# One operand of 512 columns for the high and low input parts in every second feed-forward group, and PSUM banks handed out in pairs

## The chip, the cores and the metric

The kernel runs on one core of a Trainium2 chip. The metric is the device time of one execution in microseconds (us), the median of several runs.

## The reference

Two layers of a decoder trunk with a residual h of 256 positions and 1024 channels. Each layer mixes positions in four branches, gates them and adds them to h, then runs a gated feed-forward part of 2816 channels with a causal convolution of three taps, and then adds a gated projection of a second input. Cut to what matters here:

```python
for i in range(DEPTH):                              # DEPTH = 2
    xn = rms_norm(h, norm_mix[i])
    u = xn @ w_in[i]                                # split into the inputs of four branches
    ...
    h = h + mixed @ w_out[i]
    f = causal_dwconv(rms_norm(h, norm_ffn[i]) @ w_up[i], conv_f_w[i], conv_f_b[i])   # 3 taps
    f_gate, f_val = jnp.split(f, 2, axis=-1)        # 2816 channels each
    h = h + (jax.nn.silu(f_gate) * f_val) @ w_down[i]
    e = rms_norm(p[i] @ w_ple_in[i], ple_norm[i])
    g = jax.nn.sigmoid(rms_norm(h, ple_gate_norm[i]) @ w_ple_gate[i])
    h = h + g * e
```

## The kernel before, in words

All products are matmuls in a 32-bit format with fewer bits than float32. To come near float32 each operand is split in two parts, high and low, and each product is three matmuls: high weight by high input, high weight by low input, low weight by high input. The function `mm3` (L298) issues them on L305, L306 and L307, 256 columns each where the positions are the moving columns, and `tok_unit` (L345) on L348 to L350, 512 columns each where the weights move.

The weights come from memory in pieces of 128 x 1024. `take` hands them out in the order in which they are used, three pieces ahead. ScalarE makes the high part of a piece (L232) and VectorE the low part (L233); six buffers hold split pieces, so that the high part of a new piece waits until TensorE has done with the piece six before it.

The feed-forward part has 22 groups of 128 channels for the gate and as many for the value. The loop over `g2` (L1148 on) takes two groups at a time, `q` is the group in it and `s_` chooses gate or value. `chan_unit` computes one 128x256 output with 8 x 3 = 24 matmuls, and the two outputs of a group share one PSUM bank of 512 float32 columns, a tile of `mmbank` named mm. Four such banks go round. A group's bank is evacuated by two ScalarE copies with scale and bias (L1158, the last tap of the convolution) and four VectorE products that add the other two taps (L1164). Then come a Silu (L1167) and a product (L1168), and the result is split into high and low parts (L291, L292) for the next matrix product.

The first four groups of a layer, the early ones (EARLY = 4), are computed before the scale of the norm is known; `nrm.scaled` (L479) multiplies their banks by it afterwards into SBUF, and the evacuation reads from there.

Nobody writes the order of the instructions out. The program is traced in the order of the Python code, a scheduler then orders the instructions on each engine, and semaphores are placed for each dependence. A tile is the unit of such a dependence on a buffer that is used again: whoever takes the buffer next waits until everything that reads the old tile is done.

Other places that the change touches: `evac_a` (the first branch's convolution, which is also scaled by L479), the key of the sparse branch's indexer (a unit of 40 channels, copied on L1051 and transposed on L1055), and `tok_parts` (the last product of the kernel, in three parts, each followed by a tanh on L1203).

Of the kernel before, what the change touches and what calls it, by code (L numbers as in the profile page):

```python
# [129 lines left out]
def decoder_kernel(ctx: ExitStack, tc: tile.TileContext, w_dram, x_dram, xt_dram, p_dram, vec_dram, row_dram,  # L130
# [10 lines left out]
    RAW_BUFS, SPLIT_BUFS, LEAD, NBIG = 5, 6, 3, 43  # L141
# [12 lines left out]

    def st(shape, tag, bufs=1, dtype=F32):
        return sm.tile(shape, dtype, name=nm("s"), tag=tag, bufs=bufs)

    def mmbank():
        return ps.tile([P, 2, S], F32, name=nm("mm"), tag="mm", bufs=4)
# [127 lines left out]
    def split(dst, src, scale=1.0):  # L287

        hi, lo = dst
        if scale == 1.0:  # L290
            A.activation(hi, src, AF.Copy)  # L291
            V.tensor_tensor(lo, src, hi.bitcast(F32), op=ALU.subtract)  # L292
        else:
            A.activation(hi, src, AF.Copy, scale=scale)
            V.scalar_tensor_tensor(lo, src, scale, hi.bitcast(F32), op0=ALU.mult, op1=ALU.subtract)

    def mm3(out, wl, xs, c0, first, last):
# [3 lines left out]
        for k in range(nk):  # L301
            xh, xl = xs[k]
# [5 lines left out]

    def ktiles(pairs):
        return [(pairs[k // 2][0][:, k % 2, :], pairs[k // 2][1][:, k % 2, :]) for k in range(2 * len(pairs))]  # L310
# [9 lines left out]
    def chan_banks(nb, nrm):  # L320


        banks = [mmbank() for _ in range(nb)]
        ws = take(2 * nb)
        for k0 in (0, KD // 2):
# [3 lines left out]
            for i, bank in enumerate(banks):  # L329
# [6 lines left out]
    def tok_unit(xk, npieces, after={}):  # L336


        outs = [mmbank().rearrange("p a b -> p (a b)") for _ in range(2)]
# [61 lines left out]
    class Norm:  # L401
# [11 lines left out]
        def split(self, i, src, js=(0, 1)):  # L413

            if 0 in js:
                self.xs.append((bt(dtype=F32R), bt(dtype=F32R)))
            hi, lo = self.xs[i]
# [143 lines left out]
    for l in range(L):  # L561
# [45 lines left out]
        else:  # L607
            bbanks = [mmbank() for _ in range(2)]
# [9 lines left out]
        xsk = ktiles(nrm.xs)  # L618
        for c in range(len(bbanks), 4):
            bank = mmbank()  # L620
# [44 lines left out]
        def side_d():  # L665
# [111 lines left out]
            od = [(bt(dtype=F32R), bt(dtype=F32R)) for _ in range(2)]  # L777
# [43 lines left out]
        def side_c():  # L821
# [94 lines left out]
            oc = [(bt(dtype=F32R), bt(dtype=F32R)) for _ in range(2)]  # L916
# [40 lines left out]
        def side_a():  # L957
            oa = []
            o_pairs[0] = oa
            for i in range(2):  # L960
# [24 lines left out]
                hl = (bt(dtype=F32R), bt(dtype=F32R))  # L985
# [20 lines left out]
        def side_b():  # L1006
# [13 lines left out]
            for i in range(2):  # L1020
# [5 lines left out]
                hl = (bt(dtype=F32R), bt(dtype=F32R))  # L1026
# [11 lines left out]
        for fn in (evac_a, evac_ga):  # L1038
            for i in range(2):
                bank = mmbank()  # L1040
# [7 lines left out]
        bank = mmbank()  # L1048
# [33 lines left out]
        def turn_mixed(n):  # L1082
            for i in range(2):
# [5 lines left out]
                hl = (bt(dtype=F32R), bt(dtype=F32R))  # L1089
# [54 lines left out]
        fk = ktiles(nrm.xn())  # L1144
        for g2 in range(NG // 2):
            cf = st([P, 4, S], "e4", 2)
            pair = bt()
            for q in range(2):  # L1148
                g = 2 * g2 + q
                if g < EARLY:  # L1150
                    bank = nrm.scaled(early[g])
                else:
                    bank = mmbank()
# [15 lines left out]
            hl = (bt(dtype=F32R), bt(dtype=F32R))  # L1169
            split(hl, pair)  # L1170
            hid.append(hl)
# [137 lines left out]
```

## Time and profile before

| | before |
|---|---|
| median of 3 runs | 1031.39 us (1031.32 to 1031.87) |
| the profiled execution's own time | 1031.66 us |
| its span | 1029.9 us |
| TensorE busy | 1023.2 us, 99% |
| VectorE busy | 832.9 us, 81% |
| ScalarE busy | 691.0 us, 67% |
| granted TensorE clock | 1.000 |

The span is the time from the first to the last instruction of the profiled execution; its own time is a little longer than that. Busy times are sums of the durations of instructions. The matmuls of TensorE overlap, so its busy share says that it always had work, not how fast the work went. In the profile PE is TensorE, DVE VectorE, ACT ScalarE, POOL GpSimd and SP the engine that issues the transfers.

### The profile page before, as it was taken

Reading aid. Unit: us, or ns where it says so; the run is one execution under the profiler, and the core shown is the slowest. Engines: PE = TensorE matmul, PEld = TensorE weight load, DVE = VectorE, ACT = ScalarE, POOL = GpSimd, SP = SyncE. Lnnn points to the kernel's source line nnn. Section 1 sums busy time; section 2 is a strip of 40 time slices with the busy share of each in tenths; the row PEclk is TensorE's granted clock in tenths of the full one; section 3 lists DMA queues with packets and bytes.
Section 4 is the critical chain, followed back from the end, with each engine's and each line's share of the span. In section 5 each row is a group of like instructions: output and inputs, shape, how many; then the busy total and the mean of one; then the engine's idle time right before and its main releaser. Section 6 shows DMA issues by size and latency. Waiting matters only on the chain.

```text
span 1029.9 us, 16561 instructions
## 1 busy us (share of the span) xinstructions
PE 1023.2 (99%) x6124; PEld 901.0 (87%) x6124; DVE 832.9 (81%) x1526; ACT 691.0 (67%) x1190; POOL 0.2 (0%) x4
## 2 busy tenths in 40 slices
PE   9999999999999999999999999999999999999998
PEld 9988878887889999988899887888888899999887
DVE  7898999977869988765676989999688899877454
ACT  8688685977467766554766886868774676665443
POOL 0000000000000000000000000000000000000000
PEclk9999999999999999999999999999999999999999
DMA  8665844553538566476553656445446465665551
GB/s 290 231 207 167 269 142 144 184 164 107 211 101 308 159 204 192 144 259 188 186 176 124 213 172 216 141 148 179 147 137 210 144 205 178 188 186 183 191 160 41
DMA packets 53936, 185.30 MB, mean 180 GB/s; under 512 B 6112, under 2 KB 7904, under 8 KB 53856
## 3 DMA queue, kind: packets, MB, share of 16 engines
q1 hardware_dynamic: 53712, 184.25, 55.7%
q8 instruction: 48, 0.79, 0.3%
q14 instruction: 32, 0.26, 0.1%
q10 hardware_dynamic: 144, 0.00, 0.0%
HBM read 183.18 MB, written 1.05 MB: 179 GB/s over the span
## 4 chain that ended last, share of the span: by engine, by line
PE 96%; ACT 2%; DVE 1%; DMA 1%; SPq 0%; issue 0%; ACTq 0%
PE mm L348 18%; PE mm L349 18%; PE mm L350 18%; PE mm L307 11%; PE mm L305 11%; PE mm L306 11%; PE mm L371 1%; PE sp L439 1%; PE sp L873 1%; PE sp L729 1%; PE sp L789 1%; PE sp L903 1%; DMA raw<-in_w_dram 1%; ACT b L921 0%; ACT hi L232 0%; PE sp L847 0%
## 5 line engine op out<-in xcount | busy, mean ns | idle before, releaser
L232 ACT ACTIVATE hi<-raw 128x1024 fp32r<-128x1024 f32 (+1 forms) x342 | 354.9, 1048 | 210.8 <-PE mm L350 126.6
L233 DVE TENSOR_TENSOR lo<-raw,hi 128x1024 fp32r<-128x1024 f32 (+1 forms) x342 | 410.0, 1207 | 102.1 <-ACT hi L232 99.7
L348 PE MATMUL mm<-hi,b 128*128 128x512 f32 x848 | 337.5, 399 | 0.1
L349 PE MATMUL mm<-lo,b 128*128 128x512 f32 x848 | 331.1, 391 | 0.0
L350 PE MATMUL mm<-hi,b 128*128 128x512 f32 x848 | 330.2, 390 | 0.0
L305 PE MATMUL mm<-b,hi 128*128 128x256 f32 x976 | 276.5, 285 | 0.5 <-ACT hi L232 0.3
L307 PE MATMUL mm<-b,lo 128*128 128x256 f32 x976 | 275.7, 283 | 0.2 <-DVE lo L233 0.2
L306 PE MATMUL mm<-b,hi 128*128 128x256 f32 x976 | 275.7, 283 | 0.0
L348 PEld LDWEIGHTS mm<-hi,b 128*128 128x128 f32 x848 | 159.2, 188 | 35.8 <-issue 1.8
L350 PEld LDWEIGHTS mm<-hi,b 128*128 128x128 f32 x848 | 159.2, 188 | 33.7
L305 PEld LDWEIGHTS mm<-b,hi 128*128 128x128 f32 x976 | 186.8, 192 | 1.4 <-DVE b L428 0.6
L307 PEld LDWEIGHTS mm<-b,lo 128*128 128x128 f32 x976 | 186.9, 192 | 0.6 <-DVE lo L233 0.6
L306 PEld LDWEIGHTS mm<-b,hi 128*128 128x128 f32 x976 | 187.0, 192 | 0.3 <-DVE b L429 0.2
L349 PEld LDWEIGHTS mm<-lo,b 128*128 128x128 f32 x848 | 159.5, 188 | 31.5 <-issue 0.5
L1002 DVE SCALAR_TENSOR_TENSOR b<-s,vec,b 128x256 f32<-128x256 f32 x240 | 105.4, 477 | 0.0
L1164 DVE SCALAR_TENSOR_TENSOR s<-mm,vec,s 128x255 f32<-128x255 f32 (+1 forms) x144 | 59.7, 473 | 6.0 <-ACT s L1158 6.0
L291 ACT ACTIVATE b<-b 128x512 fp32r<-128x512 f32 x40 | 25.0, 626 | 21.8 <-DVE b L1168 19.1
L1158 ACT ACTIVATE s<-mm,vec 128x256 f32<-128x256 f32 x72 | 36.2, 553 | 2.7 <-PE mm L307 2.7
L292 DVE TENSOR_TENSOR b<-b,b 128x512 fp32r<-128x512 f32 x40 | 27.4, 687 | 12.6 <-ACT b L291 12.6
L479 DVE TENSOR_TENSOR b<-mm,s 128x512 f32<-128x512 f32 x24 | 16.3, 684 | 11.1 <-PE mm L307 11.0
L1167 ACT ACTIVATE s<-s 128x256 f32<-128x256 f32 x44 | 17.8, 410 | 9.7 <-DVE s L1164 9.6
L882 ACT ACTIVATE s<-sp,s,s 128x128 f32<-128x128 f32 (+1 forms) x32 | 16.0, 513 | 12.5 <-DVE s L878 6.2
(224 smaller groups left out, 779.4 us busy)
## 6 DMA issues: line engine op xcount, KB each, us to landing
raw<-in_w_dram SPq DMA_DIRECT2D x334, 512.0 KB, 4.2
raw<-in_w_dram SPq DMA_DIRECT2D x8, 256.0 KB, 4.6
b<-in_x_dram SPq DMA_DIRECT2D x8, 128.0 KB, 4.5
b<-in_lru_dram SPq DMA_DIRECT2D x4, 256.0 KB, 4.8
h<-in_xt_dram SPq DMA_DIRECT2D x4, 256.0 KB, 6.6
gain<-in_gain_dram SPq DMA_DIRECT2D x2, 512.0 KB, 6.1
out_dram<-h SPq DMA_DIRECT2D x3, 256.0 KB, 2.3
row<-in_row_dram SPq DMA_DIRECT2D x2, 272.0 KB, 5.4
```

Source lines behind the costliest of these rows:

```text
L232: A.activation(hi[:, cs], raw[:, cs], AF.Copy)
L233: last_lo[0] = V.tensor_tensor(lo[:, cs], raw[:, cs], hi[:, cs].bitcast(F32), op=ALU.subtract).ins
L292: V.tensor_tensor(lo, src, hi.bitcast(F32), op=ALU.subtract)
L305: T.matmul(out, a, xh, start=first and k == 0, stop=False)
L306: T.matmul(out, a, xl, start=False, stop=False)
L307: T.matmul(out, b, xh, start=False, stop=last and k == nk - 1)
L348: T.matmul(outs[b], xk[k][0][:, bs], wh[:, kk, :], start=k == 0, stop=False)
L349: T.matmul(outs[b], xk[k][0][:, bs], wl[:, kk, :], start=False, stop=False)
L350: T.matmul(outs[b], xk[k][1][:, bs], wh[:, kk, :], start=False, stop=last)
L1002: V.scalar_tensor_tensor(t, ypad[:, c, d:d + S], w[:, 31 * c + d:31 * c + d + 1], t, op0=ALU.mult, op1=ALU.add)
L1158: A.activation(cf[:, 2 * q + s_, :], bank[:, s_, :], AF.Identity, scale=w[:, 3 * c + 2:3 * c + 3], bias=bb[:, c:c + 1])
L1164: V.scalar_tensor_tensor(t, bank[:, s_, :S - d], w[:, 3 * c + 2 - d:3 * c + 3 - d], t, op0=ALU.mult, op1=ALU.add)
```

## The change

PSUM tiles for products are now pairs of banks: `mmbanks` returns the two halves of a tile of two banks and the tile itself, and two such tiles go round instead of four single banks. Every place that took banks now takes halves of pairs; two groups of the feed-forward part share a pair.

`two(True)` puts the high and low parts of an input side by side in one tile, so that they can move as one operand of 512 columns (128 x 2 x 256). From the third pass of the loop on, every second pass (g2 = 2, 4, 6, 8, 10) is `apart`: `mm3_apart` multiplies the high weight by the 512 columns into a whole bank (L322), the high input's product in its first half and the low input's in its second, and the low weight by the high input's 256 columns into the first half (L323). Two matmuls replace three. The two halves are added afterwards: ScalarE copies the second halves out of the pair (L1194), VectorE adds the first halves (L1195). In these passes ScalarE also makes the second tap's product (L1201), which one VectorE add per pass brings in (L1212); two VectorE products per group stay (L1206). `finish_group` runs Silu, product and split for both groups of a pass at once, and after the next pass's first group has been evacuated. Lines in the changed kernel: the weight pieces are split on L241 and L242, groups on L300 and L301, `mm3` is on L314 to L316, `tok_unit` on L364 to L366, `nrm.scaled` on L496, the copies with bias on L1198, the indexer's copy and transpose on L1070 and L1074.

```diff
-    RAW_BUFS, SPLIT_BUFS, LEAD, NBIG = 5, 6, 3, 43
+    RAW_BUFS, SPLIT_BUFS, LEAD, NBIG, NPAIR = 5, 6, 3, 36, 4
...
+    def two(paired=False):
+
+        if not paired:
+            return bt(dtype=F32R), bt(dtype=F32R)
+        t = big.tile([P, 2, 2, S], F32R, name=nm("b2"), tag="big2", bufs=NPAIR)
+        return t[:, 0], t[:, 1], t
...
-    def mmbank():
-        return ps.tile([P, 2, S], F32, name=nm("mm"), tag="mm", bufs=4)
+    def mmbanks():
+
+        t = ps.tile([P, 2, 2, S], F32, name=nm("mm"), tag="mm", bufs=2)
+        return t[:, 0], t[:, 1], t
...
+    def mm3_apart(out, wl, xs):
+
+        wh, wlo = wl
+        for k, (xh, _, xhl) in enumerate(xs):
+            T.matmul(out, wh[:, k, :], xhl, start=k == 0, stop=False)
+            T.matmul(out[:, 0, :], wlo[:, k, :], xh, start=False, stop=k == len(xs) - 1)
...
     def tok_unit(xk, npieces, after={}):
-        outs = [mmbank().rearrange("p a b -> p (a b)") for _ in range(2)]
+        outs = [flat(bank) for bank in mmbanks()[:2]]
...
         pcs = take(npieces)
+        halves = mmbanks()
         for b, c, n in ((0, 0, 512), (1, 0, 256), (1, 256, 256)):
-            bank = mmbank().rearrange("p a b -> p (a b)")[:, :n]
+            bank = flat(mmbanks()[0] if c == 0 and b == 0 else halves[c // 256])[:, :n]
...
                 V.tensor_tensor(xf, xf, self.rs2, op=ALU.mult)
-                hl = (bt(dtype=F32R), bt(dtype=F32R))
+                hl = two(True)
                 split(hl, xf)
...
         for fn in (evac_a, evac_ga):
+            both = mmbanks()
             for i in range(2):
-                bank = mmbank()
+                bank = both[i]
                 for j in range(2):
                     chan_unit(bank, j, xsk, 1)
                     pump()
...
-        bank = mmbank()
+        bank = mmbanks()[0]
         chan_unit(bank, 0, xsk, 1)
         t = st([40, S], "ikc", 1)
         A.activation(t, bank[0:40, 0, :], AF.Copy)
...
         for g in range(1, EARLY):
-            bank = mmbank()
+            if g % 2 == 0:
+                early += mmbanks()[:2]
             for s_ in range(2):
-                chan_unit(bank, s_, xsk, 1)
-            early.append(bank)
+                chan_unit(early[g], s_, xsk, 1)
         fk = ktiles(nrm.xn())
+
+        def finish_group(cf):
+            gv = cf.rearrange("p (q s) t -> p s q t", s=2)
+            sl, pair = bt(), bt()
+            A.activation(sl, gv[:, 0], AF.Silu)
+            V.tensor_tensor(pair, sl, gv[:, 1], op=ALU.mult)
+            hl = two()
+            split(hl, pair)
+            hid.append(hl)
+
+        waiting = None
         for g2 in range(NG // 2):
+            apart = 2 * g2 >= EARLY and g2 % 2 == 0
             cf = st([P, 4, S], "e4", 2)
-            pair = bt()
+            t1 = st([P, 4, S], "e4d", 2) if apart else None
             for q in range(2):
                 g = 2 * g2 + q
                 if g < EARLY:
-                    bank = nrm.scaled(early[g])
+                    u = nrm.scaled(early[g])
                 else:
-                    bank = mmbank()
+                    if apart or q == 0:
+                        banks = mmbanks()
                     for s_ in range(2):
-                        chan_unit(bank, s_, fk, 1)
+                        if apart:
+                            mm3_apart(banks[s_], take(1)[0], fk)
+                        else:
+                            chan_unit(banks[q], s_, fk, 1)
+                    u = banks[q]
+                if apart:
+                    u = bt()
+                    A.activation(u, banks[2][:, :, 1, :], AF.Copy)
+                    V.tensor_tensor(u, banks[2][:, :, 0, :], u, op=ALU.add)
                 for s_ in range(2):
                     c = g + s_ * NG
-                    A.activation(cf[:, 2 * q + s_, :], bank[:, s_, :], AF.Identity, scale=w[:, 3 * c + 2:3 * c + 3],
+                    A.activation(cf[:, 2 * q + s_, :], u[:, s_, :], AF.Identity, scale=w[:, 3 * c + 2:3 * c + 3],
                                  bias=bb[:, c:c + 1])
-                for d in (1, 2):
+                    if apart:
+                        A.activation(t1[:, 2 * q + s_, :], u[:, s_, :], AF.Copy, scale=w[:, 3 * c + 1:3 * c + 2])
+                for d in (2,) if apart else (1, 2):
                     for s_ in range(2):
                         c = g + s_ * NG
                         t = cf[:, 2 * q + s_, d:]
-                        V.scalar_tensor_tensor(t, bank[:, s_, :S - d], w[:, 3 * c + 2 - d:3 * c + 3 - d], t,
+                        V.scalar_tensor_tensor(t, u[:, s_, :S - d], w[:, 3 * c + 2 - d:3 * c + 3 - d], t,
                                                op0=ALU.mult, op1=ALU.add)
-                sl = st([P, S], "tb", 2)
-                A.activation(sl, cf[:, 2 * q, :], AF.Silu)
-                V.tensor_tensor(pair[:, q, :], sl, cf[:, 2 * q + 1, :], op=ALU.mult)
-            hl = (bt(dtype=F32R), bt(dtype=F32R))
-            split(hl, pair)
-            hid.append(hl)
+                if waiting is not None:
+                    finish_group(waiting)
+                    waiting = None
+            if apart:
+                V.tensor_tensor(cf[:, :, 1:], cf[:, :, 1:], t1[:, :, :S - 1], op=ALU.add)
+            waiting = cf
+        finish_group(waiting)
```

TensorE, before, at the border of two groups in the steady part of the first layer's feed-forward loop. mm_3764 is the bank of a group, mm_3834 that of the next one; hi and lo are the two parts of a weight piece.

```order
L306 MATMUL mm_3764<-b_3557,hi_3690 128x256
L307 MATMUL mm_3764<-b_3556,lo_3691 128x256
L305 MATMUL mm_3834<-b_3541,hi_3720 128x256 [waits DVE_49,Activation_49]
L306 MATMUL mm_3834<-b_3542,hi_3720 128x256
L307 MATMUL mm_3834<-b_3541,lo_3721 128x256
```

The next group begins in another of the four banks, whose evacuation lies further back.

TensorE, of the change, at a like place. mm_3683 is the pair of an ordinary pass, mm_3826 and mm_3888 are the pairs of the first and second group of an apart pass, and mm_3888 has the same two banks as mm_3683.

```order
L314 MATMUL mm_3683<-b_671_3518,hi_3685 128x256
L315 MATMUL mm_3683<-b_671_3518,hi_3685 128x256
L316 MATMUL mm_3683<-b_671_3518,lo_3686 128x256
L323 MATMUL mm_3826<-b_670_3514,lo_3760 128x256
L322 MATMUL mm_3826<-b_670_3514,hi_3759 128x512
L323 MATMUL mm_3826<-b_670_3514,lo_3760 128x256
L322 MATMUL mm_3826<-b_671_3518,hi_3759 128x512
L323 MATMUL mm_3826<-b_671_3518,lo_3760 128x256
L322 MATMUL mm_3826<-b_671_3518,hi_3759 128x512
L323 MATMUL mm_3826<-b_671_3518,lo_3760 128x256
L322 MATMUL mm_3888<-b_668_3506,hi_3789 128x512 [waits DVE_49,Activation_49]
L323 MATMUL mm_3888<-b_668_3506,lo_3790 128x256
```

Seven matmuls of the first apart group now stand between the end of the ordinary pass and the matmul that takes its banks again.

VectorE, of the change, at the same place: s_3682 is the ordinary pass's result, and L1206 with mm_3683 as its source are the products of its second group.

```order
L242 TENSOR_TENSOR lo_3891<-raw_3889,hi_3890 128x1024 [waits DMAHW7_49,PE_49,Activation_49]
L242 TENSOR_TENSOR lo_3913<-raw_3911,hi_3912 128x1024 [waits DMAHW0_49,PE_49,Activation_49]
L1206 SCALAR_TENSOR_TENSOR s_3682<-mm_3683,vec_75,s_3682 128x255 [waits Activation_49]
L1206 SCALAR_TENSOR_TENSOR s_3682<-mm_3683,vec_75,s_3682 128x255
L1206 SCALAR_TENSOR_TENSOR s_3682<-mm_3683,vec_75,s_3682 128x254 [waits DVE_49] x2
L1195 TENSOR_TENSOR b_3871<-mm_3826,b_3871 128x512 [waits Activation_49]
L1169 TENSOR_TENSOR b_3881<-b_3880,s_3682 128x512 [waits DVE_49,Activation_49]
```

The low parts of two weight pieces stand ahead of the four products, as the low part of a piece did before, and the products are now what the pair's next user waits for.

VectorE, of the change, at the entry of the first layer's loop: mm_3384 is the pair of the third and fourth early groups, mm_3565 that of the first apart group.

```order
L496 TENSOR_TENSOR b_3539<-mm_3384,s_3322 128x512 [waits PE_49]
L242 TENSOR_TENSOR lo_3630<-raw_3628,hi_3629 128x1024 [waits DMAHW7_49,Activation_49]
L1206 SCALAR_TENSOR_TENSOR s_3538<-b_3539,vec_75,s_3538 128x255 [waits Activation_49] x2
L1206 SCALAR_TENSOR_TENSOR s_3538<-b_3539,vec_75,s_3538 128x254 [waits DVE_49] x2
L1169 TENSOR_TENSOR b_3548<-b_3547,s_3521 128x512 [waits Activation_49]
L242 TENSOR_TENSOR lo_3652<-raw_3650,hi_3651 128x1024 [waits DMAHW0_49,PE_49,Activation_49]
L301 TENSOR_TENSOR b_3552<-b_3548,b_3551 128x512 [waits Activation_49]
L496 TENSOR_TENSOR b_3555<-mm_3384,s_3322 128x512
L1195 TENSOR_TENSOR b_3610<-mm_3565,b_3610 128x512 [waits Activation_49]
```

The two scalings of one pair now stand nine instructions apart, and the pair is free only after the second.

## Rows read from the trace of the kernel before

**Rows 1.** Page: busy time of the engines; two of the lines in 40 slices.
```profile
PE 1023.2 (99%) x6124; PEld 901.0 (87%) x6124; DVE 832.9 (81%) x1526; ACT 691.0 (67%) x1190; POOL 0.2 (0%) x4
...
PE   9999999999999999999999999999999999999998
...
PEclk9999999999999999999999999999999999999999
```
**Rows 2.** Page: the chain that ended last, by engine.
```profile
PE 96%; ACT 2%; DVE 1%; DMA 1%; SPq 0%; issue 0%; ACTq 0%
```
**Rows 3.** TensorE's waits: us in total, times, longest; the first row.
```profile
PE sp L205 <- DVE eps L184: 1.0, 1, 1.0
```
**Rows 4.** Windows of both feed-forward parts: us, PE, PEld, DVE, ACT, POOL, PEclk, DMA.
```profile
311.00:460.00 149.00, 149.00 (x1131) 144.00 (x1131) 122.95 (x198) 98.01 (x142) 0.00 (x0) 1.00 0.64 208
808.00:958.00 150.00, 149.84 (x1165) 145.91 (x1164) 124.54 (x199) 97.24 (x150) 0.00 (x0) 1.00 0.59 182
```
**Rows 5.** Timeline of TensorE in the feed-forward loop: start, us, instruction.
```profile
399.72 0.28 PE L306 MATMUL mm<-b,hi 128*128 128x256 f32 x1
...
400.92 0.28 PE L307 MATMUL mm<-b,lo 128*128 128x256 f32 x1
...
408.24 0.28 PE L305 MATMUL mm<-b,hi 128*128 128x256 f32 x1
```
**Rows 6.** Timeline of TensorE after the loop, 512 columns.
```profile
449.69 0.39 PE L348 MATMUL mm<-hi,b 128*128 128x512 f32 x1
...
456.49 0.39 PE L348 MATMUL mm<-hi,b 128*128 128x512 f32 x1
```
**Rows 7.** Timeline of ScalarE at the end of a group.
```profile
408.32 1.06 ACT L232 ACTIVATE hi<-raw 128x1024 fp32r<-128x1024 f32 x1 [1.66 <-PE mm L306]
409.28 1.01 ACT L1158 ACTIVATE s<-mm,vec 128x256 f32<-128x256 f32 x2
```
**Rows 8.** Timeline of VectorE at the ends of groups.
```profile
403.94 1.65 DVE L1164 SCALAR_TENSOR_TENSOR s<-mm,vec,s 128x255 f32<-128x255 f32 x4 [0.22 <-ACT s L1158]
...
409.41 1.23 DVE L233 TENSOR_TENSOR lo<-raw,hi 128x1024 fp32r<-128x1024 f32 x1 [1.22 <-ACT hi L232]
410.55 1.65 DVE L1164 SCALAR_TENSOR_TENSOR s<-mm,vec,s 128x255 f32<-128x255 f32 x4
```
**Rows 9.** Groups of ScalarE by line and shape, 356 to 452 us.
```profile
L232 ACT ACTIVATE hi<-raw 128x1024 fp32r<-128x1024 f32 x34 | 35.5, 1055 | 21.5 <-PE mm L306 17.4 <-DMA raw<-in_w_dram 3.2 <-PE mm L350 0.8
...
L291 ACT ACTIVATE b<-b 128x512 fp32r<-128x512 f32 x9 | 5.6, 629 | 8.2 <-DVE b L1168 8.2
```
**Rows 10.** Groups of VectorE by line and shape, 356 to 452 us.
```profile
L233 DVE TENSOR_TENSOR lo<-raw,hi 128x1024 fp32r<-128x1024 f32 x36 | 43.4, 1220 | 10.6 <-ACT hi L232 10.0
L1164 DVE SCALAR_TENSOR_TENSOR s<-mm,vec,s 128x255 f32<-128x255 f32 x28 | 12.2, 476 | 4.4 <-ACT s L1158 4.4
...
L292 DVE TENSOR_TENSOR b<-b,b 128x512 fp32r<-128x512 f32 x9 | 6.1, 689 | 4.2 <-ACT b L291 4.2
```
**Rows 11.** Timeline of VectorE at the entry of the feed-forward loop.
```profile
334.70 0.69 DVE L292 TENSOR_TENSOR b<-b,b 128x512 fp32r<-128x512 f32 x1 [0.70 <-ACT b L291]
```
**Rows 12.** Timelines of TensorE and VectorE at the convolution branch's first bank.
```profile
36.66 0.28 PE L305 MATMUL mm<-b,hi 128*128 128x256 f32 x1
...
36.86 0.69 DVE L479 TENSOR_TENSOR b<-mm,s 128x512 f32<-128x512 f32 x1 [2.76 <-PE mm L307]
```
**Rows 13.** Timelines of ScalarE and TensorE around the indexer's key.
```profile
78.78 1.28 ACT L970 ACT_TABLE_LOAD   x1
...
84.62 0.38 ACT L1051 ACTIVATE s<-mm 40x256 f32<-40x256 f32 x1
...
82.10 0.40 PE L348 MATMUL mm<-hi,b 128*128 128x512 f32 x1
```
**Rows 14.** Timelines of ScalarE and TensorE in the last product.
```profile
1022.69 0.47 ACT L1203 ACTIVATE b<-mm,s 128x256 f32<-128x256 f32 x1 [2.18 <-PE mm L371]
...
1022.37 0.40 PE L371 MATMUL mm<-hi,b 128*128 128x256 f32 x2
```

More of the change, by code (lines that the diff above doesn't have):

```diff
@@ L287, in split @@
     def split(dst, src, scale=1.0):
-        hi, lo = dst
+        hi, lo = dst[:2]
         if scale == 1.0:
@@ L301, in mm3 @@
         for k in range(nk):
-            xh, xl = xs[k]
+            xh, xl = xs[k][:2]
             a = wh[:, k, c0:c0 + P]
@@ L307, in mm3 @@
             T.matmul(out, b, xh, start=False, stop=last and k == nk - 1)
+    def mm3_apart(out, wl, xs):
[3 more added lines that the diff above has]
+            T.matmul(out[:, 0, :], wlo[:, k, :], xh, start=False, stop=k == len(xs) - 1)
     def ktiles(pairs):
-        return [(pairs[k // 2][0][:, k % 2, :], pairs[k // 2][1][:, k % 2, :]) for k in range(2 * len(pairs))]
+        return [(hl[0][:, j, :], hl[1][:, j, :]) + tuple(t[:, :, j, :] for t in hl[2:]) for hl in pairs for j in range(2)]
     def chan_unit(bank, j, xs, npieces):
@@ L320, in chan_banks @@
     def chan_banks(nb, nrm):
-        banks = [mmbank() for _ in range(nb)]
+        banks = [bank for _ in range((nb + 1) // 2) for bank in mmbanks()[:2]]
         ws = take(2 * nb)
@@ L328, in chan_banks @@
             xs = ktiles(nrm.xs)
-            for i, bank in enumerate(banks):
+            for i, bank in enumerate(banks[:nb]):
                 for q in range(2):
@@ L415, in split @@
             if 0 in js:
-                self.xs.append((bt(dtype=F32R), bt(dtype=F32R)))
-            hi, lo = self.xs[i]
+                self.xs.append(two())
+            hi, lo = self.xs[i][:2]
             xf = bt() if self.keep else None
@@ L607, in decoder_kernel @@
         else:
-            bbanks = [mmbank() for _ in range(2)]
+            bbanks = list(mmbanks()[:2])
             for k in range(KD):
@@ L618, in decoder_kernel @@
         xsk = ktiles(nrm.xs)
+        later = mmbanks()
         for c in range(len(bbanks), 4):
-            bank = mmbank()
+            bank = later[c % 2]
             for j in range(2):
@@ L776, in side_d @@
             yield from weave(heads(b) for b in range(2))
-            od = [(bt(dtype=F32R), bt(dtype=F32R)) for _ in range(2)]
+            od = [two(True) for _ in range(2)]
             o_pairs[3] = od
@@ L915, in side_c @@
             V.reciprocal(mo, mo)
-            oc = [(bt(dtype=F32R), bt(dtype=F32R)) for _ in range(2)]
+            oc = [two() for _ in range(2)]
             o_pairs[2] = oc
@@ L984, in side_a @@
                 V.tensor_tensor(tr, ga[i], tr, op=ALU.mult)
-                hl = (bt(dtype=F32R), bt(dtype=F32R))
+                hl = two(True)
                 split(hl, tr)
@@ L1025, in side_b @@
                 A.activation(t, y[i], AF.Silu)
-                hl = (bt(dtype=F32R), bt(dtype=F32R))
+                hl = two()
                 split(hl, t)
@@ L1088, in turn_mixed @@
                         T.transpose(bank[:, 2 * j + b, :], mixed[b, n][:, c:c + P], ident)
-                hl = (bt(dtype=F32R), bt(dtype=F32R))
+                hl = two()
                 split(hl, bank.rearrange("p (j b) c -> p j (b c)", j=2))
@@ L1139, in decoder_kernel @@
         for g in range(1, EARLY):
-            bank = mmbank()
+            if g % 2 == 0:
+                early += mmbanks()[:2]
             for s_ in range(2):
-                chan_unit(bank, s_, xsk, 1)
-            early.append(bank)
+                chan_unit(early[g], s_, xsk, 1)
         fk = ktiles(nrm.xn())
+        def finish_group(cf):
[3 more added lines that the diff above has]
+            V.tensor_tensor(pair, sl, gv[:, 1], op=ALU.mult)
+            hl = two()
+            split(hl, pair)
+            hid.append(hl)
+        waiting = None
         for g2 in range(NG // 2):
+            apart = 2 * g2 >= EARLY and g2 % 2 == 0
             cf = st([P, 4, S], "e4", 2)
-            pair = bt()
+            t1 = st([P, 4, S], "e4d", 2) if apart else None
             for q in range(2):
```

2 lines of the change are left out of this document (removed).

## The prediction

> **What bounds the kernel now.** I read the page's first two parts first: TensorE is busy 99% of the span, VectorE 81%, ScalarE 67%, and the granted clock is in its top tenth in all 40 slices, its level of 2.4 GHz [rows 1]. The chain that ended last agrees: 96% of it is TensorE [rows 2]. Then I looked for gaps: the largest entry of TensorE's waits is 1.0 us, once, ahead of the first matmuls [rows 3]. In the feed-forward stretches of the two layers TensorE works 149.00 of 149 us and 149.84 of 150, while VectorE has 122.95 and 124.54 us of work and ScalarE 98.01 and 97.24 [rows 4]. So the reader is to see two things: time can be won only by giving TensorE less to do, and any instruction that makes TensorE wait adds its whole wait, since there is no slack in the chain to take it. The question is what the order of the changed kernel makes TensorE wait for.
>
> **What it removes.** A matmul of 256 columns follows the one before it after 0.120 us (10 steps in 1.20 us) [rows 5], one of 512 after 0.2267 us (30 steps in 6.80 us) [rows 6]. Two of 256 cost 0.2400, so a merged pair saves 0.0133 us. Five groups of each layer are taken apart, each with 2 x 2 units of 8 pieces, so 5 x 32 x 2 = 320 pairs merge: **-4.3 us**. The Trainium skill ("TensorE: Matmul & The Clock Gate", section "Wait — 56ns, not 53.3ns?") gives some 2.5 ns as the fixed part of a matmul; by that the gain would be 0.8 us. The rows decide here: 0.120 and 0.2267 leave a fixed part of 13.3 ns.
>
> **What it adds beside TensorE.** An apart group gets an extra copy and an add of 128x512 per half, two scaled copies of 128x256 per half and one add of 4x255, and loses four of its eight VectorE products. With ScalarE's 1.055 us per weight piece and 0.63 us per 128x512 [rows 9], and 0.5 us per 128x256 [rows 7], the apart group has about 4 x 1.055 + 2 x (0.63 + 4 x 0.505) + 0.63 + 0.63 = 10.8 us of ScalarE work (reads outside the bank taken at the bank's price, an estimate). VectorE: 4 x 1.22 + 2 x 0.69 + 4 x 0.476 + 1.22 (for the add of 1020 columns, by the weight piece of 1024) + 0.69 + 0.69 = 10.7 us [rows 10]. TensorE has 32 x 0.3467 = 11.1 us. An ordinary group has 11.5 us of TensorE, about 7.5 of ScalarE and 9.6 of VectorE; two neighbours together have 22.6 against 18.3 and 20.3. So these edits cost nothing on average, hidden by TensorE; without that cover ScalarE would just equal it within the apart group.
>
> **What it moves: the wait behind an ordinary group (W2).** Before, four banks are handed out one at a time, and a bank comes free when its own evacuation ends. Now there are two pairs, and a pair comes free as a whole. In the order, the first 512-column matmul of an apart second half (mm_3888) goes into the banks of the ordinary group (mm_3683), and between the last matmul of that group and it stand only seven matmuls: 4 x 0.120 + 3 x 0.2267 = 1.16 us. It waits for the last L1206 on that group. What must run in that time? The order puts the high part of a weight piece (hi_3912) ahead of the group's two copies on ScalarE, and the low part (lo_3913) ahead of the four products on VectorE; hi_3912 itself waits for nearly the last matmul of the group, since it needs that matmul's weight buffer. This is the same sequence that the trace of before shows, where nobody waits for it: the high part starts at 408.32 and the two copies at 409.28 [rows 7], the low part at 409.41, the four products from 410.55 for 1.65 us, that is to 412.20 [rows 8]. In before the next unit's first matmul started at 408.24 [rows 5], into another bank. On that clock the changed kernel's seven matmuls take TensorE to 409.40, and the pair is free at 412.20 plus about 0.04 us for the signal (estimate, from the 0.04 between the end of the matmul and the start at 408.32): a stall of 2.84 us. It comes with every apart group but the first of a layer, 4 per layer, 8 in all: **+22.7 us**. Bounds: products at their single price (4 x 0.476 = 1.90 instead of 1.65, [rows 10]) that also wait 0.22 for a copy, as at 403.94 [rows 8], give 3.3 each, 26.4; if high and low part were not in front, the copies would begin at 408.44, the products at about 409.0, and the pair would be free at 410.68: 1.28 each, 10.2. I take 2.84, since the order shows the very sequence. What is queued behind the waiting matmul is all of TensorE's work; nothing else is late next, as ScalarE and VectorE catch up meanwhile and the other pair's evacuation is done by the time.
>
> **The wait ahead of the ordinary second half (W1).** Its first matmul now shares a pair with the first half and waits for that half's evacuation. 25 matmuls of the apart unit stand between, 13 of 512 at most: 4.3 to 4.4 us, against the 3.9 us sequence above, so 0 to 0.5 each, 8 times. I take 0.05: **+0.4** (0 to 4).
>
> **The entry of the feed-forward part (E).** The first apart group's second half takes the pair of the third and fourth early groups, and waits for both to be scaled. Behind TensorE's end of that pair VectorE has in its order L496, a low part, four products, a 128x512 product, a low part, the low part of a group and L496 again: 0.69 + 1.22 + 1.65 + 0.69 + 1.22 + 0.69 + 0.69 = 6.85 [rows 8, 10, 12], plus the 0.70 us that VectorE waits for ScalarE's half of a split [rows 11], 7.55 in all. The cover is 32 matmuls, 5.55 us. Stall 2.0, two layers: **+4.0** (0 if the scaling starts before the pair's end, 6 with a late table load).
>
> **Smaller sharings.** *A, the convolution branch:* the second unit pair's bank is the same tile as the first's, and no matmul stands between; it waits for L496. In before L479 ran from 36.86 for 0.69 us, while the next unit's first matmul started at 36.66 [rows 12]: 37.55 + 0.04 - 36.66 = 0.93, two layers, **+1.9** (1.4 to 3). *C, the indexer's key:* its transpose now stands two 512-column matmuls (0.45 us) behind the end of its unit. In before the copy it needs ran at 84.62, for 0.38 us, behind a busy ScalarE, and the next matmul after the unit stood at 82.10 [rows 13]. Ahead of the copy the new order has the table load of 1.28 us and two sigmoids fewer (these by the copy's 0.38, an estimate), about 2.0 us: 82.61 + 0.38 + 0.04 - 82.55 = 0.5 us, two layers, **+1.0** (0.4 to 5, the latter with ScalarE as late as before). *D, the tail:* the third part's matmuls now wait for the tanh of the second part, which shares the pair: it starts at 1022.69 for 0.47, and the matmul slot is the second of two from 1022.37, 1022.49 [rows 14]: **+0.7**.
>
> **Sum.** 22.7 + 0.4 + 4.0 + 1.9 + 1.0 + 0.7 - 4.3 = +26.4 us. The profiled execution took 1031.66 us (span 1029.9, the rest lies outside it), which is 0.27 above the median of the runs, 1031.39. So 1058.1 against its own time, **1057.8 us** as a median.
>
> **The rivals.** 0.2% of this kernel, 2.1 us, is about what a measurement can tell from no change.
> *Faster, the waits do not bite:* if the pair's evacuation ends within the 1.16 us of cover, W2 is gone, and with it goes the case for the others: 1031.4 - 4.3 = 1027.1. It decides at 1.16 us from matmul end to release. Against it: the same sequence takes 3.9 us in the trace, more than three times that [rows 7, 8]. The Trainium skill ("PSUM — Partial Sum Buffer", section "Summary: rules for kernel authors") would have the guard by bank, and reads go to another bank than the matmuls; by that rule mm_3888 could start in the first bank earlier, and the time would lie near this rival. The order guards by pair and waits for the last product. Chance 0.03.
> *A short W2:* high and low part are done before the group's end, the stall is 1.28 us each: 12.5 us less, 1045.3. For it: ScalarE idles 30% of the stretch [rows 4]. Against it: the weight buffer that hi_3912 needs is freed only at the group's end. Chance 0.08.
> *All upper bounds:* 26.4 + 4 + 6 + 3 + 5 + 0.7 - 4.3 = 40.8, 1072. For it: ScalarE equals TensorE in an apart group, so a late piece is not caught up. Chance 0.05.
> *The clock falls:* before, TensorE never idles in these stretches and the granted clock is 1.00 [rows 4]; now it idles eight times for some 2.8 us. If after each of these one unit (8 x 0.3467 = 2.77 us) ran at 1.2 GHz, it would take twice as long: 22 us more, 1080. No row of before speaks for a fall, as none has such a gap. The Trainium skill ("TensorE: Matmul & The Clock Gate", section "A second HAM failure mode: psum-queue depth-cycling") tells of a kernel whose clock went to and fro for short idling between groups of matmuls as its banks came free; no run here shows it yet. Chance 0.05.
>
> **How the numbers follow.** The forecast has 0.79. The range 1044 to 1070 holds it with its bounds and the short W2; left out are the faster case, the clock and the sum of all upper bounds, 0.13. Faster by over 0.2%: 0.03; within 0.2%: 0.02, for a W2 that costs just what the merge gives; slower: 0.95.
>
> **What the profile after would show.** TensorE's waits should list L322 waiting for VectorE's L1206, 8 times, 20 to 26 us, the longest near 3; L322 behind L496 some 2 us at the entry and L314 behind L496 0.9 in the convolution branch; a share of TensorE near 96% instead of 99. TensorE's steps should be 0.2267 + 0.120 in an apart unit. A granted clock below 1.00 in the feed-forward stretches would show the last rival. The prediction is wrong if L322's waits come to under 10 us, which would mean that the high and low parts ran before the group's end, or if the waits are as forecast and the time is not, which would mean that another engine or the clock sets it.

## The result and the profile after

The changed kernel takes 1090.38 us (median of 4 runs, 1088.20 to 1091.19), the kernel before 1031.63 us in the same series: ratio 1.0564, 95% interval 1.0548 to 1.0581. The change makes it 5.6% slower. The forecast was slower as well, by 26.4 us; it is 58.8.

The page of the changed kernel, the two lines in slices and the chain by engine, beside [rows 1, 2]:

```profile
PE 1041.8 (96%) x5804; PEld 897.0 (82%) x5804; DVE 841.5 (77%) x1494; ACT 715.7 (66%) x1228; POOL 0.2 (0%) x4
...
PE   9999999999999888899999999999999998888998
...
PEclk9999999999999999999999989999999999999999
...
PE 87%; ACT 7%; DVE 5%; issue 1%; DMA 1%; SPq 0%; ACTq 0%; DVEq 0%
```

The span is 1087.8 us, 57.9 more than before, and the profiled execution took 1089.69. TensorE has 320 matmuls fewer and yet more busy time; that is the first hint that some of them were slower. ScalarE and VectorE hold 12% of the chain, where they had 3%. TensorE's waits in the changed kernel (us in total, times, longest), beside [rows 3]:

```profile
PE mm L322 <- DVE s L1206: 22.1, 8, 2.8
PE mm L364 <- ACT b L676: 4.2, 2, 3.0
PE mm L322 <- DVE b L496: 3.7, 2, 1.9
PE mm L314 <- DVE b L496: 1.8, 2, 0.9
PE mm L364 <- ACT hi L241: 1.7, 1, 1.7
PE mm L315 <- DVE b L446: 1.7, 3, 0.9
PE mm L364 <- ACT b L1098: 1.3, 2, 0.7
PE sp L214 <- DVE eps L193: 1.0, 1, 1.0
PE mm L314 <- ACT b L1246: 0.9, 1, 0.9
```

The eight waits of L322 are the ones called W2. One of them in the timelines of TensorE, ScalarE and VectorE (start, duration, instruction; in brackets the idle time ahead of it):

```profile
363.70 0.28 PE L323 MATMUL mm<-b,lo 128*128 128x256 f32 x1
366.74 0.47 PE L322 MATMUL mm<-b,hi 128*128 128x512 f32 x1 [2.76 <-DVE s L1206]
...
367.62 0.63 PE L322 MATMUL mm<-b,hi 128*128 128x512 f32 x1
...
370.19 0.63 PE L322 MATMUL mm<-b,hi 128*128 128x512 f32 x1
...
371.15 0.40 PE L322 MATMUL mm<-b,hi 128*128 128x512 f32 x1
...
372.89 0.39 PE L322 MATMUL mm<-b,hi 128*128 128x512 f32 x1
```

```profile
362.71 1.06 ACT L241 ACTIVATE hi<-raw 128x1024 fp32r<-128x1024 f32 x1 [1.82 <-PE mm L315]
363.68 1.00 ACT L1198 ACTIVATE s<-mm,vec 128x256 f32<-128x256 f32 x2
```

```profile
363.81 1.23 DVE L242 TENSOR_TENSOR lo<-raw,hi 128x1024 fp32r<-128x1024 f32 x1 [1.66 <-ACT hi L241]
364.95 1.64 DVE L1206 SCALAR_TENSOR_TENSOR s<-mm,vec,s 128x255 f32<-128x255 f32 x4
```

It is the sequence of [rows 7, 8], step for step: high part, copies, low part, four products, 362.71 to 366.59 (3.88 us, as at 408.32 to 412.20 before), and TensorE starts 0.15 us behind its end. What stands next in TensorE's timeline was not in the sum: from 367.62 to 370.19 four merged pairs take 0.6425 us each; from 371.15 to 372.89 five take 0.348 each again. The windows of this place and of the longest wait, with the granted clock in the column behind POOL's:

```profile
363.50:366.70 3.20, 0.48 (x4) 0.16 (x2) 2.90 (x6) 3.01 (x6) 0.00 (x0) 1.00 0.55 177
366.70:371.20 4.50, 4.46 (x17) 3.86 (x18) 3.66 (x6) 2.64 (x6) 0.00 (x0) 0.62 0.48 175
...
624.30:627.40 3.10, 0.20 (x2) 0.00 (x0) 1.73 (x4) 3.10 (x8) 0.00 (x0) 0.90 0.97 363
627.40:634.00 6.60, 6.52 (x16) 4.31 (x17) 2.66 (x4) 3.49 (x11) 0.00 (x0) 0.53 0.04 16
```

Behind the idle time TensorE works at 1.2 GHz, the lower of its two levels, for a while. All eight W2 waits, one of the two at the loop's entry and the one of 3.0 us at 624 were followed by such a stretch, a fall of the clock, in this execution. The mean granted clock is 0.983.

**Where 57.9 us went.** The waits add 41.6 us by the full list less 1.0 for L214 and 1.0 for those that before had too: 39.6. A wait costs a little more than its idle time, since the last matmul's 0.28 us no longer overlap with the next one: 363.70 to 366.74 is 3.04, less the usual 0.12 is 2.92, 0.16 above the listed 2.76; with some 25 waits 4.0. The clock: 1.7% of 1087.8 us are missing at half speed, so 37 us were spent at 1.2 GHz, and a pair that takes 0.353 us took 0.6425, so 45% of that is lost, 16.7 us. That is an estimate for all ten falls of this execution. Behind the wait above, eight pairs stand between 366.74 and 371.15, 4.41 us where eight of 0.353 are 2.82: 1.59 us for one wait, 12.7 for the eight of W2. The merge gives 2.1 back (next section). 39.6 + 4.0 + 16.7 - 2.1 = 58.2.

### The profile page after: what moved, and what is told of

It reads as the page before. It is cut to its first block, busy times and chain, and to the rows that moved or that the text cites. A ratio compares the mean times of both kernels' runs of the same rounds, so it can differ in the third digit from the quotient of the medians.

```text
span 1087.8 us, 15885 instructions
## 1 busy us (share of the span) xinstructions
PE 1041.8 (96%) x5804; PEld 897.0 (82%) x5804; DVE 841.5 (77%) x1494; ACT 715.7 (66%) x1228; POOL 0.2 (0%) x4
## 4 chain that ended last, share of the span: by engine, by line
PE 87%; ACT 7%; DVE 5%; issue 1%; DMA 1%; SPq 0%; ACTq 0%; DVEq 0%
PE mm L364 17%; PE mm L366 17%; PE mm L365 17%; PE mm L322 7%; PE mm L314 7%; PE mm L315 6%; PE mm L316 6%; PE mm L323 3%; ACT hi L241 3%; DVE lo L242 1%; DVE s L1206 1%; PE mm L388 1%; PE sp L456 1%; PE sp L891 1%; PE sp L747 1%
## 5 line engine op out<-in xcount | busy, mean ns | idle before, releaser
L242 DVE TENSOR_TENSOR lo<-raw,hi 128x1024 fp32r<-128x1024 f32 (+1 forms) x342 | 410.5, 1207 | 159.1 <-ACT hi L241 157.9
L241 ACT ACTIVATE hi<-raw 128x1024 fp32r<-128x1024 f32 (+1 forms) x342 | 355.8, 1049 | 248.4 <-PE mm L366 134.1
L364 PE MATMUL mm<-hi,b 128*128 128x512 f32 x848 | 338.9, 400 | 7.2 <-ACT b L676 4.2
L365 PE MATMUL mm<-lo,b 128*128 128x512 f32 x848 | 331.8, 391 | 0.8 <-DVE lo L242 0.8
L366 PE MATMUL mm<-hi,b 128*128 128x512 f32 x848 | 332.1, 392 | 0.0
L364 PEld LDWEIGHTS mm<-hi,b 128*128 128x128 f32 x848 | 159.9, 189 | 43.3 <-ACT b L676 4.6
L314 PE MATMUL mm<-b,hi 128*128 128x256 f32 x656 | 187.2, 286 | 4.1 <-DVE b L496 1.8
L366 PEld LDWEIGHTS mm<-hi,b 128*128 128x128 f32 x848 | 159.6, 188 | 34.1
L315 PE MATMUL mm<-b,hi 128*128 128x256 f32 x656 | 185.5, 283 | 1.7 <-DVE b L446 1.7
L365 PEld LDWEIGHTS mm<-lo,b 128*128 128x128 f32 x848 | 160.0, 189 | 32.7 <-DVE lo L242 1.1
L316 PE MATMUL mm<-b,lo 128*128 128x256 f32 x656 | 185.7, 284 | 0.4 <-DVE lo L242 0.4
L322 PE MATMUL mm<-b,hi 128*128 128x512 f32 x320 | 127.8, 434 | 25.8 <-DVE s L1206 22.1
L314 PEld LDWEIGHTS mm<-b,hi 128*128 128x128 f32 x656 | 125.5, 191 | 7.4 <-issue 2.3
L315 PEld LDWEIGHTS mm<-b,hi 128*128 128x128 f32 x656 | 125.5, 191 | 2.4 <-DVE b L446 2.3
L316 PEld LDWEIGHTS mm<-b,lo 128*128 128x128 f32 x656 | 125.5, 191 | 1.0 <-DVE lo L242 0.9
L322 PEld LDWEIGHTS mm<-b,hi 128*128 128x128 f32 x320 | 66.8, 209 | 44.5 <-ACT hi L241 21.4
L323 PE MATMUL mm<-b,lo 128*128 128x256 f32 x320 | 96.1, 300 | 0.0
L323 PEld LDWEIGHTS mm<-b,lo 128*128 128x128 f32 x320 | 67.2, 210 | 0.0
L1198 ACT ACTIVATE s<-b,vec 128x256 f32<-128x256 f32 x56 | 32.1, 590 | 4.5 <-DVE b L1195 3.2
L300 ACT ACTIVATE b<-b 128x512 fp32r<-128x512 f32 x40 | 24.8, 622 | 11.0 <-DVE b L1169 8.7
L1206 DVE SCALAR_TENSOR_TENSOR s<-b,vec,s 128x254 f32<-128x254 f32 (+1 forms) x72 | 30.7, 476 | 1.6 <-ACT s L1198 1.5
```

Of the source, the lines that this page charges most:

```text
L241: A.activation(hi[:, cs], raw[:, cs], AF.Copy)
L242: last_lo[0] = V.tensor_tensor(lo[:, cs], raw[:, cs], hi[:, cs].bitcast(F32), op=ALU.subtract).ins
L314: T.matmul(out, a, xh, start=first and k == 0, stop=False)
L315: T.matmul(out, a, xl, start=False, stop=False)
L316: T.matmul(out, b, xh, start=False, stop=last and k == nk - 1)
L322: T.matmul(out, wh[:, k, :], xhl, start=k == 0, stop=False)
```

## The experiments

The theory: the merge itself gains about 2 us; the pairing makes all the waits; and some of them cost a second time, because the clock falls behind them. The main rival: the apart groups cost by themselves, through ScalarE's extra work or through a clock that their wider matmuls bring down.

| kernel | median us | ratio to before, 95% | clock of the profiled execution |
|---|---|---|---|
| changed kernel | 1090.38 | 1.0548 to 1.0581 | 0.983 |
| pairs, no merge | 1083.47 | 1.0489 to 1.0525 | 0.991 |
| merge, single banks | 1030.46 | 0.9980 to 0.9997 | 0.999 |
| single banks, no merge | 1031.93 | 0.9990 to 1.0008 | 0.999 |

**Pairs alone.** No group is apart.

```diff
-            apart = 2 * g2 >= EARLY and g2 % 2 == 0
+            apart = False
```

> The changed kernel with no group apart: banks in pairs and the late finishing of a group stay, every product is three matmuls of 256 columns again. Theory (the pairing makes the waits, the merged operand makes none): in the feed-forward loop every ordinary group now waits for the evacuation of its own pair, with 2.8 to 3.0 us of matmuls to cover 3.9 us, so some 30 waits of about 1 us, 25 to 40 us, beside some 15 us outside the loop; granted clock near 1.00, since no single wait comes near 2.8 us; 1070 to 1090 us. Rival (the apart groups' own work, matmuls of 512 columns and more ScalarE work, is the cost): only the 15 us outside the loop remain, 1045 to 1050 us.

Measured 1083.47 us. The pairing alone costs nearly all of it; the rival's 1045 to 1050 is far off. The waits, however, are fewer and longer than expected, and the clock, expected near 1.00, was 0.991:

```profile
PE mm L314 <- DVE s L1206: 18.5, 12, 2.7
PE mm L314 <- DVE b L496: 5.3, 4, 1.8
PE mm L364 <- ACT b L676: 4.2, 2, 3.0
```

The windows of its two longest waits behind L1206 in the first layer, each with the stretch behind it:

```profile
354.00:356.70 2.70, 0.04 (x1) 0.00 (x0) 2.70 (x6) 2.70 (x6) 0.00 (x0) 1.00 0.63 165
356.70:361.20 4.50, 4.41 (x37) 4.44 (x38) 3.84 (x7) 1.04 (x2) 0.00 (x0) 1.00 0.35 108
380.30:382.10 1.80, 0.09 (x1) 0.00 (x0) 1.80 (x6) 1.79 (x3) 0.00 (x0) 1.00 0.39 123
382.10:386.60 4.50, 4.42 (x24) 4.45 (x25) 3.23 (x6) 0.70 (x2) 0.00 (x0) 0.62 0.59 207
```

Behind 2.7 us of idling the clock held, behind 1.8 us it fell, and the second layer shows the same pair of sequels (1.00 from 895.90, 0.62 from 921.30). So the length of a wait alone does not decide whether the clock falls behind it.

**The merge alone.** Four single banks go round, every place takes them one at a time, and each bank of an apart group is copied and added by itself.

```diff
+    def mmbank():
+        return ps.tile([P, 2, S], F32, name=nm("mm"), tag="mm", bufs=4)
...
-        t = ps.tile([P, 2, 2, S], F32, name=nm("mm"), tag="mm", bufs=2)
-        return t[:, 0], t[:, 1], t
+        return mmbank(), mmbank()
...
-                    A.activation(u, banks[2][:, :, 1, :], AF.Copy)
-                    V.tensor_tensor(u, banks[2][:, :, 0, :], u, op=ALU.add)
+                    for s_ in range(2):
+                        A.activation(u[:, s_, :], banks[s_][:, 1, :], AF.Copy)
+                        V.tensor_tensor(u[:, s_, :], banks[s_][:, 0, :], u[:, s_, :], op=ALU.add)
```

> The merge alone: the changed kernel, but four single banks go round as before, and each bank of an apart group is copied out and added by itself, 256 columns at a time. Theory (pairing makes all the waits, and the waits make the clock fall): no wait of over 0.5 us in the feed-forward loop, granted clock 1.00, and a gain between 2.1 and 4.3 us, as the apart unit measured 0.3533 us per merged pair and piece (0.3467 was predicted) against 0.3600: 1027 to 1030 us. Rival (the apart groups' work or the wider matmuls cost, by ScalarE or by the clock): 1040 us or more, with a clock under 1.00 or waits behind L1194 or the adds.

Measured 1030.46 us, ratio 0.9988 (0.9980 to 0.9997): a little faster than before, just short of the range. TensorE's waits hold nothing of the loop any more; the rows of L366 and L365, 0.5 and 0.3, are just behind the first layer's loop:

```profile
PE sp L215 <- DVE eps L194: 1.0, 1, 1.0
PE mm L315 <- ACT hi L242: 0.6, 1, 0.6
PE mm L366 <- DVE lo L243: 0.5, 1, 0.5
PE mm L317 <- DVE lo L243: 0.5, 2, 0.2
PE mm L365 <- ACT hi L242: 0.3, 1, 0.3
```

The price of a merged pair is read from the first and the last of the 32 wide matmuls of one apart group in this kernel's timeline (L323 there), (361.68 - 350.73) / 31 = 0.3532 us:

```profile
350.73 0.40 PE L323 MATMUL mm<-b,hi 128*128 128x512 f32 x1
...
361.68 0.40 PE L323 MATMUL mm<-b,hi 128*128 128x512 f32 x1
```

Three matmuls of 256 columns took 0.3600, so the gain is 0.0068 a pair, 2.2 us for 320, half of the predicted 4.3. Such a pair takes about 0.0065 us longer than the sum of what each matmul takes among its like, 0.2267 + 0.1200. That wide and narrow alternate is not by itself the reason, since behind the wait of the changed kernel the same alternation took 0.348; what is was not settled.

**The fourth corner.** The same single banks with `apart = False`.

> Single banks and no group apart: of the change only the late finishing of a pass's two groups (one Silu, one product and one split of 128x512) and the other tiles in SBUF stay. It is the fourth corner of pairs or singles, merged or not. Theory (the merge gives about 0.0067 us for each of 320 merged pairs, 2.1 us, and the late finishing gives nothing): 1031 to 1032.5 us, so that the merge on single banks is 1 to 2 us below it. Rival (the merge gives nothing, the late finishing is what made 1030.46): 1030.0 to 1030.8 us.

Measured 1031.93 us, within the range and no different from before (0.9990 to 1.0008). The late finishing gives nothing. On single banks the merge is worth 1.5 us; on pairs it adds 6.9 us. The idle times of the two kernels with pairs sum to nearly the same, 41.6 us with the merge and 39.3 without, by their full lists. What differs is mainly the clock: by the working above, 0.983 costs 16.7 us and 0.991 some 9.

**Busy during the wait.** Needless matmuls stand ahead of the one that waits; `junk` is one of the small banks, and nothing reads it.

```diff
+                    if apart and q == 1 and g2 >= 4:
+                        junk = flat(smbank())
+                        jw = prev[0]
+                        for n in range(12):
+                            T.matmul(junk, jw[:, n % KD, :], fk[n % KD][2], start=n == 0, stop=n == 11)
...
-                            mm3_apart(banks[s_], take(1)[0], fk)
+                            prev = take(1)[0]
+                            mm3_apart(banks[s_], prev, fk)
```

> The changed kernel with twelve needless matmuls of 512 columns (2.72 us, their result is never read) put in TensorE's queue just ahead of each of the eight matmuls that wait some 2.8 us for the pair. The wait's cause and end stay, TensorE only works during it. Theory (the clock falls because TensorE idles for 2.8 us): granted clock 1.00 in the loop, and the time falls by 8 x 1.7 us to 1075 to 1079 us although there is more work. Rival (the clock falls for another reason, the wider matmuls for one): clock as before, 1089 to 1093 us. Second rival (the idling costs, not the clock): no change, 1089 to 1091 us with a clock of 1.00.

Measured 1080.02 us: 96 matmuls more, 10.4 us less. The profiled execution took 1074.86 at a clock of 0.998, the other three about 1080 at 0.992 or 0.993; where these lost their clock is not on record. In the windows of the profiled one, the wait that fell in 363.5 to 366.7 is now filled, and the granted clock behind it stays:

```profile
365.50:368.40 2.90, 2.88 (x15) 2.08 (x13) 2.90 (x6) 1.77 (x4) 0.00 (x0) 1.00 0.54 210
368.40:373.00 4.60, 4.60 (x27) 4.04 (x28) 3.93 (x7) 4.39 (x8) 0.00 (x0) 1.00 0.43 148
```

So it is the idling that lets the clock fall there, not the wide matmuls. The merge on single banks, with the same wide matmuls and no such waits, kept 0.999. The two rivals, 1089 us or more, are out. The median lies 1 us above the expected range.

**Half of the wait filled.** Six needless matmuls instead of twelve.

> As the kernel that works during the eight waits, with six needless matmuls instead of twelve, 1.36 us, so that TensorE idles about 1.4 us of each wait. Theory (an idle time of 2.8 us lets the clock fall, one near 1.4 us seldom does, as after the waits of 0.9 to 1.9 us in the changed kernel, of which one of 15 was followed by a fall): 1075 to 1083 us, like twelve. Rival (any idle time at these places lets it fall): 1088 to 1092 us.

Measured 1079.85 us, as with twelve. The waits are half as long, and the clock holds behind them (windows of one of them; L1212 is L1206 here):

```profile
PE mm L322 <- DVE s L1212: 11.0, 8, 1.4
```

```profile
367.10:368.60 1.50, 0.12 (x2) 0.09 (x1) 1.50 (x5) 1.40 (x2) 0.00 (x0) 1.00 0.46 66
368.60:373.00 4.40, 4.40 (x25) 3.85 (x26) 4.00 (x7) 3.66 (x7) 0.00 (x0) 1.00 0.47 164
```

The mean clock of this execution is 0.992 all the same, as it fell at other places. One of them is behind the first layer's loop, where TensorE waited for a weight piece, 1.7 us and then 0.8:

```profile
461.60:464.00 2.40, 1.60 (x6) 1.10 (x7) 2.37 (x3) 2.40 (x3) 0.00 (x0) 1.00 0.02 3
464.00:468.00 4.00, 4.00 (x12) 3.14 (x11) 3.86 (x4) 2.44 (x3) 0.00 (x0) 0.57 0.95 306
```

The expectation counted 15 waits of 0.9 to 1.9 us in the changed kernel. Its trace has 8 of these, and some 14 from 0.5 us on; one was followed by a fall.

**Three pairs.** Six banks for products, two for the small ones.

```diff
-        t = ps.tile([P, 2, 2, S], F32, name=nm("mm"), tag="mm", bufs=2)
+        t = ps.tile([P, 2, 2, S], F32, name=nm("mm"), tag="mm", bufs=3)
...
-        return ps.tile([P, 4, P], F32, name=nm("sp"), tag="sp", bufs=4)
+        return ps.tile([P, 4, P], F32, name=nm("sp"), tag="sp", bufs=2)
```

> The changed kernel with three pairs of banks going round instead of two, and two instead of four banks for the small products. Theory (waits come from the pair's late return, and the clock from the waits): the eight waits of 2.8 us, those at the entry of the loop and those behind the second token product go, with them the eight falls of the clock and the one at 627 us; the two waits of the convolution branch and that of the last product stay: 1030 to 1045 us, the upper end if two small banks are too few for attention. Rival (the apart groups cost by themselves): 1065 us or more.

Measured 1053.54 us, above the range. W2, the entry and L676 are gone as expected; but two small banks are too few, which the range had only as its upper end:

```profile
PE sp L865 <- ACT s L900: 6.7, 2, 3.4
PE mm L314 <- DVE b L496: 1.8, 2, 0.9
```

The clock of this execution was 0.994. About 5 of its 22.3 us above the span of before are not accounted for by its waits and its clock; these were not followed up.

**The indexer's key in a small bank.** The two waits behind L676 were not in the prediction.

```diff
-        bank = mmbanks()[0]
+        bank = flat(smbank()).rearrange("p (a b) -> p a b", a=2)
```

> The changed kernel with one unit moved: the indexer's key is summed in one of the four small banks and takes no pair. Theory (that unit uses up a whole pair for one half bank, so that the token unit behind it must wait for the evacuation of the token unit just ahead of it, L676): the two waits of 1.3 and 3.0 us of L364 behind L676 go, 4.5 us with what the pipeline loses at each, and with the longer one the fall of the clock near 627 us, 3.4 us; in all 1081 to 1085 us against 1090.4. Rival (L676 is late there anyway, for ScalarE's queue, and another instruction will wait): 1088 to 1091 us with a new wait behind ScalarE at 83 and 624 us.

Measured 1084.06 us (ratio 1.0497 to 1.0538), within the range. L676 has left the list of waits, and W2 stands as it was:

```profile
PE mm L322 <- DVE s L1206: 22.1, 8, 2.8
PE mm L322 <- DVE b L496: 4.0, 2, 2.1
```

So one unit of 40 channels that takes a whole pair costs some 5 to 6 us (6.3 by the medians, 4.8 by the ratios to before): it uses up the turn of the pair that the next token unit needs.

**More and fewer apart passes on single banks.** From the third pass on, eight passes a layer (all but the last):

```diff
-            apart = 2 * g2 >= EARLY and g2 % 2 == 0
+            apart = 2 * g2 >= EARLY and 2 * g2 + 2 < NG
```

Or four, every second one without the last:

```diff
-            apart = 2 * g2 >= EARLY and g2 % 2 == 0
+            apart = 2 * g2 >= EARLY and g2 % 2 == 0 and 2 * g2 + 2 < NG
```

> Single banks, and all passes from the third to the last but one are apart, eight of a layer instead of five; the last pass is ordinary. Theory (TensorE alone counts, 0.0067 us per merged pair, 8 x 32 x 2 = 512 pairs, and the 0.9 us of waits at the end of the first layer's loop goes with the last apart pass): 3.4 us less than the kernel before, 1027.9 to 1029 us. Rival (ScalarE, with 10.8 to 11.1 us of work for 11.3 us of TensorE per apart pass, falls behind when no ordinary pass stands between): waits of TensorE behind L242 or L1194 and 1035 us or more, with falls of the clock if they reach some 2 us.

> Single banks, apart only in the passes 2, 4, 6 and 8, the last pass ordinary. Theory: 256 merged pairs give 1.7 us, and the waits of 0.9 us at the end of the first layer's loop behind L242 and L243 are gone, since the last pass's results come earlier: 1029.7 to 1030.3 us. Rival (those waits come from the late finishing, not from the apart pass): they stay, 1030.5 to 1031.2 us.

Measured 1028.33 us with eight (ratio 0.9968, 0.9955 to 0.9980) and 1030.12 with four (0.9983, 0.9974 to 0.9992), both within their ranges. Eight passes is the fastest kernel of the study, 3.4 us below before as 512 pairs predict. The rows of the loop, 320 to 437 us of that kernel, show TensorE full with ScalarE at 84% of the time:

```profile
320.00:437.00 117.00, 117.00 (x709) 103.88 (x708) 106.74 (x171) 97.73 (x174) 0.00 (x0) 1.00 0.59 189
```

That ScalarE falls behind is refuted at this number of passes. The 0.9 us at the end of the first layer's loop came with the last apart pass: with four passes and the last one ordinary, only this is left there:

```profile
PE mm L366 <- DVE lo L243: 0.2, 1, 0.2
```

## Why the prediction was right and wrong, step by step

**What bounds the kernel** was right: TensorE had no slack, each wait came through whole. **W2** was right in place, number, releaser and size: 8 waits, 22.1 us of idle time and 23.4 with the lost overlap, against 22.7. **E** measured 3.7 (4.0 predicted), **A** 1.8 (1.9), **D** 0.6 (0.7). **W1** shows no entry; 0.4 was allowed. **Added work** beside TensorE cost nothing, as computed and as the merge on single banks shows.

**What failed first** is the clock, for which the sum had no term. It stood among the rivals with a chance of 0.05, with the words that no row of before speaks for it; a trace without a long gap could not speak against it either. Its mechanism and its place were put rightly, behind each of eight waits. Its price was too high, 22 us for these eight where they cost some 12.7: of the eight pairs behind the wait shown above, four ran at the lower level in full and two in part, not all eight. With the other two falls it is the 16.7. The rival should have had a far larger chance. In the trace, 0.62 was granted behind a wait of 2.76 us and 1.00 again later. The Trainium skill ("TensorE: Matmul & The Clock Gate", section "A second HAM failure mode: psum-queue depth-cycling") tells of a kernel that cycles through PSUM banks and whose clock goes to and fro as TensorE idles briefly between groups of matmuls; the trace agrees. The prediction had also named the sign that came: the waits are as forecast and the time is not. The time with this rival as it was priced, 1080, would have been 10 us low.

**What failed second** is the list of sharings. **C** had the wrong releaser: TensorE waited for the token unit's evacuation (L676, 4.2 us), not for the transpose, since the indexer's unit takes a whole pair; 1.0 was predicted. The waits behind L1098, L1246, L445, L446, L606 and behind the weight pieces (L241, L242), some 8 us together, were not in the sum at all: I looked for places where the code shares a pair, not for every place where a rotation of four had become one of two. For the weight pieces that is not the reason, or not alone: with three pairs their waits were still 1.7 and 0.8 us. With the overlap lost at each wait, 4.0, and the 2.2 that the merge lacks, this is the other half of the missing 32 us.

**The merge** was mis-sized: 2.1 to 2.2 us instead of 4.3. The step 0.2267 + 0.1200 was read from matmuls among their like; in a steady run the pair took 0.3532. The Trainium skill ("TensorE: Matmul & The Clock Gate", section "Wait — 56ns, not 53.3ns?") has a smaller fixed part, by which the gain would be 0.8, an estimate; that is not met either.

**The rival "waits do not bite"** is refuted by W2; **"a short W2"** too, as the high and low part ran exactly ahead of the products.

## What to carry to other kernels

When buffers of a rotation are made larger and fewer, list every user of the rotation, and for each the work between the end of the old user and the start of the next against the evacuation's whole sequence, the weight preparation ahead of it in the queues included. On an engine without slack a wait can cost twice: its own length, and the clock behind it. Here eight waits of 2.8 us were each followed by a fall, with pairs alone two of 2.7 us were not and two of 1.8 us were; so give the fall a place in the range, and do not rule it out or count on it by a wait's length alone. A merge of matmuls can be had without pairing their banks, and needs a price from a steady run of the same matmuls.

## What was not expected of the hardware

The same wait need not have the same sequel. The wait of 3.0 us at L364 was followed by a granted clock of 0.53 in the changed kernel; with twelve needless matmuls in the loop it was as long, and the clock held:

```profile
620.20:623.20 3.00, 0.11 (x1) 0.00 (x0) 1.64 (x4) 3.00 (x7) 0.00 (x0) 1.00 0.93 367
623.20:630.00 6.80, 6.72 (x28) 5.05 (x29) 4.38 (x6) 6.22 (x24) 0.00 (x0) 1.00 0.02 8
```

A longer wait need not be the worse one: with pairs alone the clock held behind 2.7 us and fell behind 1.8, in both layers. Of the two waits of 1.9 us at the loop's entry in the changed kernel, one was followed by a fall. The eight waits that all were come at like places, 27.3 to 27.4 us apart within a layer, so they are hardly eight independent cases. Executions of one kernel thus differ more than before: 1074.86 to 1080.24 us with clocks of 0.998 to 0.992 for the kernel with twelve needless matmuls, where all runs of the kernel before lie within 1.3 us. What decides between them was not settled.

A wide and a narrow matmul in steady alternation cost 6 to 7 ns more than the two do among their like (0.3532 us against 0.3467). Behind a wait the same pair took 0.348, and why was not settled either.
